# Both parts of each mixer weight kept in DRAM for the second token half, and W_down added up into four output blocks

## The chip, the cores and the metric

The kernel runs on one core of a Trainium2 chip. The metric is device time in microseconds (us); lower is better. PE is TensorE (matmuls), DVE is VectorE, ACT is ScalarE, POOL is GpSimd, and SP is SyncE, which here only issues DMA transfers, one after the other, in a fixed order.

## The reference

One decoder layer on x of 1024 tokens by 1024 columns, in float32:

```python
h    = rms_norm(x, norm_mix_pre)
proj = h @ w_in                      # 1024 x 2568: u, v (gMLP), z, xBC (Mamba-2), dt
y_a  = u * (W_s @ layer_norm(v) + b) # per chunk of 128 tokens, after gelu
y_b  = ssd(conv(xBC), dt) * silu(z)  # chunked scan over 128-token chunks, then normed
x    = x + rms_norm(concat[y_a, y_b] @ w_out, norm_mix_post)
f    = relu(rms_norm(x, norm_ffn_pre) @ w_up) ** 2     # 1024 x 4096
x    = x + rms_norm(f @ w_down, norm_ffn_post)
```

## The kernel before

Every float32 product is made of three matmuls in the faster type float32r (`mm3`): an operand is cut into a high part (an ACT cast) and a low part (a subtraction, on POOL or DVE; `split`), and high x high, high x low and low x high are added up in PSUM.

**Mixer (0 to about 440 us).** Tokens go in two halves of 512, H0 and H1. Weights come in units of 512 KB. The list `units` has 28 mixer units (8 for xBC, 4 for z, 4 for v, 4 for u, 8 for `w_out`) and names each of them twice, once for each half; then 16 units of `w_up`. `load_unit` (line 216) loads a unit into one of two staging tiles `ws`, ACT casts it to `wh`, POOL subtracts to `wl`, and both stand in a ring of five (`N_SPLIT`) until PE has used them. The second use of a unit repeats all of this. The scan part works chunk by chunk: `ssd_a` loads a tile `gg` of decay sums by SP (`gg<-acd`, line 582), DVE, ACT and DVE turn it into a mask, and PE uses it in `ssd_c`. PE fills the time between chunks with the z, v and u products.

**W_up (440 to 750 us)** and **W_down (750 to 1018 us)** use Strassen's scheme with seven products instead of eight for blocks of 2 x 2. W_down works on 7 groups of `f` rows in stages `SG` of one, two, two and two groups. In a stage the seven products come in the order `ORD`; each is added up in one of two sets of four PSUM banks (`pd`), and product 2 goes on top of product 1, product 3 on top of product 5 (`MORE`). After each product `flush` (line 1184) adds the bank set to one of seven SBUF blocks `acc` of 128 x 2048. Behind the last stage, further adds between these blocks make four output blocks out of seven.

**Tail (1018 us to the end).** The eighth group is multiplied plainly, for 8 token tiles (t) in two column halves each, 12 matmuls into a bank `pl`: DVE adds `pl` to `acc`, ACT squares and sums, POOL multiplies by the norm weight, DVE runs a chain of small operations for 1/rms (`chain`), and `finish` scales, adds x and writes out. `TAIL` sets which tiles share a chain: three pairs, then two single tiles. `some(k)` sets how many steps of the chain and finish of an earlier tile are issued after each `pl` add.

All engines run their instructions in order. In the mixer the order on each engine is set by a scheduler at build time; the tail is in written order.

Of the kernel before, what the change touches and what calls it, by code (L numbers as in the profile page):

```python
# [8 lines left out]
F32 = mybir.dt.float32  # L9
# [6 lines left out]
P = 128  # L16
# [40 lines left out]
def hymba_kernel(ctx, tc, x, norm_mix_pre, w_in, gm_ln_w, gm_ln_b, gm_w_s, gm_b_s,  # L57
# [151 lines left out]
    def stage_unit(i):  # L209
# [3 lines left out]
        loads.append(nc.sync.dma_start(st, src).ins.name)  # L213
        staged[i] = st, shape

    def load_unit(eng=None):
        i = state["load"]
        if i >= len(units):
            return
        state["load"] += 1  # L220
        if i not in staged:
            stage_unit(i)
        st, shape = staged.pop(i)
        wh = wpool.tile(shape, F32R, tag="wh", bufs=N_SPLIT, name=f"wh{i}")
        wl = wpool.tile(shape, F32R, tag="wl", bufs=N_SPLIT, name=f"wl{i}")
        split(wh, wl, st, eng)
        ready.append((wh, wl))

    def next_unit(ahead=2, eng=None):
        i = state["use"]  # L230
# [114 lines left out]
    def step(op):  # L345
        kind, arg = op[0], op[1:]
        t = int(arg[0]) if arg else 0
        if kind == "S":
            ssx[t] = sumsq(x0[t], f"ssx0{t}")
        elif kind == "R":  # L350
            chains = [rstd_steps(ssx[int(c)], D) for c in arg]
            for c, steps in zip(arg, chains):
                rx[int(c)] = next(steps)
            while chains:
                chains = [c for c in chains if next(c, 0) is None]
        elif kind == "N":
            dve.scalar_tensor_tensor(x0[t], x0[t], rx[t], wpre, op0=ALU.mult, op1=ALU.mult)
        elif kind == "M":
            for q in range(2):
                qs = slice(q * 512, (q + 1) * 512)  # L360
                pool.tensor_tensor(x0[t][:, qs], x0[t][:, qs], wpre[:, qs], op=ALU.mult)
        elif kind == "C":
            act.activation(x0[t], x0[t], AF.Copy, scale=rx[t])
        elif kind == "T":
            for q in range(2):
                ps = (mm_bank, ss_bank, mi_bank)[PRO_BANK[t]](f"tx0{t}_{q}")
                psx[t, q] = ps.rearrange("p (k c) -> p k c", c=P)
                for k in range(4):
                    c0 = (4 * q + k) * P
                    pe.transpose(psx[t, q][:, k, :], x0[t][:, c0:c0 + P], ident)  # L370
        elif kind in "HL":
            q = int(arg[1])
            h, l = [y[:, 4 * q:4 * q + 4, t * P:(t + 1) * P] for y in hT]
            if kind == "H":
                act.copy(h, psx[t, q])
            else:
                dve.tensor_tensor(l, psx[t, q], f(h), op=ALU.subtract)
        elif kind == "W":
            st, shape = staged.pop(t)
            wh = wpool.tile(shape, F32R, tag="wh", bufs=N_SPLIT, name=f"wh{t}")  # L380
            wl = wpool.tile(shape, F32R, tag="wl", bufs=N_SPLIT, name=f"wl{t}")
            act.copy(wh, st)
            units01[t] = wh, wl, st
        elif kind == "V":
            wh, wl, st = units01[t]
            pool.tensor_tensor(wl, st, f(wh), op=ALU.subtract)
            ready.append((wh, wl))
            state["load"] += 1
        else:
            small_setup()  # L390
# [482 lines left out]
    def sub(eng, out_, a, b):  # L873
        tt(eng, out_, a, b, ALU.subtract)
# [219 lines left out]
    now["nwp"] = pool_of(ctx, "nw2")  # L1094
    pctx2 = stack()
    psum2 = pool_of(pctx2, "psum2", space=bass.MemoryType.PSUM)
    accs = {i: apool.tile([P, 4, 512], F32, name=f"acc{i}") for i in range(1, 8)}
    last = N_GROUP - 1


    SG = [(0,), (1, 2), (3, 4), (5, 6), (last,)]
    sg_of = {g: (n, gs.index(g)) for n, gs in enumerate(SG) for g in gs}
    ORD = (1, 5, 2, 3, 6, 7, 4)
    MORE = {2: 1, 3: 5}
    raws, wts, pcs = {}, {}, {}
    wr_loads = []

# [20 lines left out]
    def w_block(g, key):  # L1128
        if key[0] == "b":
            return rows(g, int(key[1]) - 1)[:, :, int(key[2]) - 1, :]  # L1130
        if (g, key) not in wts:
            one, two = {"t1": ("b12", "b11"), "t2": ("b22", "t1"), "t3": ("b22", "b12"),
                        "t4": ("t2", "b21")}[key]
            a_, b_ = w_block(g, one), w_block(g, two)
            t_ = a_ if key == "t4" else dpool.tile([P, 2, 512], F32, tag="wt", bufs=4, name=f"w{key}_{g}")
            sub(dve, t_, a_, b_)
            wts[g, key] = t_
        return wts[g, key]
# [3 lines left out]
    frs = {}  # L1142

    def f_load(name, src):
        frs[name] = stage.tile([P, 2, 512], F32, tag="ws", bufs=N_STAGE, name="fr" + name)
        nc.sync.dma_start(frs[name], src)

    def f_piece(name, tags=("fh", "fl"), bufs=3):
        fr = frs[name]
        hl = piece([P, 2, 512], "f" + name) if tags is None else \  # L1150
            tuple(dpool.tile([P, 2, 512], F32R, tag=t_, bufs=bufs, name=f"f{i}" + name)
                  for i, t_ in enumerate(tags))
        split(*hl, fr)
        return hl
# [26 lines left out]
    floads = [lambda g=g, i=i: d_load(g, i) for n, g, i in seq]  # L1181
    floads += [lambda i=i: last_load(i) for i in range(4)]

    def flush(n, i, ps):
        a_ = accs
        if n == 0:
            act.copy(a_[i], ps)
            return
        if n == len(SG) - 2 and i == 4:
            sub(dve, a_[4], a_[4], ps)  # L1190
            return
        add(dve, a_[i], ps, a_[i])
        if n < len(SG) - 2:
            return
        if i == 6:
            add(dve, a_[6], a_[6], a_[1])
            add(dve, a_[3], a_[3], a_[6])
        elif i == 7:
            add(dve, a_[7], a_[7], a_[6])
            sub(dve, a_[4], a_[7], a_[4])  # L1200
            add(dve, a_[5], a_[5], a_[7])

    w_load(0, 0)
    floads[0]()
# [5 lines left out]
    for m, (n, g, i) in enumerate(seq):  # L1210
        gs = SG[n]
        k = m - seq.index((n, gs[0], ORD[0]))
        if k == len(gs):
            w_load(n + 1, 0)
        elif k == 5 * len(gs) + 1:
            w_load(n + 1, 1)
        floads[m + 3]()
        preps[m + 2]()
        (fh, fl), (h, l) = pcs[g, i]
        if g == gs[0]:  # L1220
            banks[i] = banks[MORE[i]] if i in MORE else \
                psum2.tile([P, 4, 512], F32, tag="pd", bufs=2, name=f"pd{n}_{i}")
        ps = banks[i]
        for t in range(4):
            tsl = slice(t * P, (t + 1) * P)
            for q in range(2):
                mm3(ps[:, t, :], fh[:, q, tsl], fl[:, q, tsl], h[:, q, :], l[:, q, :],
                    g == gs[0] and q == 0 and i not in MORE, g == gs[-1] and q == 1,
                    skip_group_check=i in MORE)
        if g == gs[-1]:  # L1230
            flush(n, i, ps)
    for m in range(len(seq) + 2, len(preps)):
        if m + 1 < len(preps):
            floads[m + 1]()
# [4 lines left out]
    psum3 = pool_of(ctx, "psum3", space=bass.MemoryType.PSUM)  # L1239

    def acc(t, dh):
        return accs[((2, 3), (4, 5))[t // 4][dh]][:, t % 4, :]

    xqs, sss, chains, rs = [], {}, {}, {}
    TAIL = ((0, 1), (2, 3), (4, 5), (6,), (7,))

    def chain(ts):

        nsmall[0] += 1
        w = len(ts)  # L1250
        v = const.tile([P, w], F32, tag=f"tv{w}", bufs=2, name=f"tv{nsmall[0]}")
        dve.tensor_tensor(v, sss[ts][:, :, 0], sss[ts][:, :, 1], op=ALU.add)
        yield
        steps = rstd_steps(v, D)
        r = next(steps)
        for j, t in enumerate(ts):
            rs[t] = r[:, j:j + 1]
        yield from steps
# [38 lines left out]
    for ts in TAIL:  # L1297
        ss = sss[ts] = const.tile([P, len(ts), 2], F32, tag=f"st{len(ts)}", bufs=4, name=f"ssy{ts[0]}")
        for j, t in enumerate(ts):
            tsl = slice(t * P, (t + 1) * P)  # L1300
            for dh in range(2):
                ds_ = slice(dh * 512, (dh + 1) * 512)
                a_ = acc(t, dh)
                ps = psum3.tile([P, 512], F32, tag="pl", bufs=8, name=f"pl{t}{dh}")
                for i in range(4):
                    mm3(ps, ffs[i][0][:, tsl], ffs[i][1][:, tsl], us[i][0][:, dh, :],
                        us[i][1][:, dh, :], i == 0, i == 3)
                add(dve, a_, ps, a_)
                junk = now["tok"].tile([P, 512], BF16, tag="junk", bufs=1, name=f"yj{t}{dh}")
                act.activation(junk, a_, AF.Square, accum_out=ss[:, j, dh:dh + 1])  # L1310
                pool.tensor_tensor(a_, a_, wfpost[:, ds_], op=ALU.mult)
                some(6 if len(ts) > 1 else 12)
        todo.append(chain_op(ts))
        for t in ts:
            todo += [finish_op(t, 0), finish_op(t, 1)]
# [29 lines left out]
```

## Time and profile before

| | |
|---|---|
| Three timed runs | 1083.33, 1087.95, 1088.11 us; median 1087.95 |
| Profiled execution, own time | 1084.19 us |
| Its span, first to last instruction | 1082.5 us (so 1.7 us lie around it) |
| Busy share of PE, DVE, ACT, POOL | 95%, 70%, 46%, 36% |
| Mean granted TensorE clock | 0.983 |
| DMA moved | 172.40 MB, mean 159 GB/s |

Busy time is what an engine spent in instructions. PE is busy nearly all the time, so what counts is where PE stands still, what it waits for there, and what happens behind its last matmul. The granted clock is a share of TensorE's full 2.4 GHz: 0.50 in a stretch is the level of 1.2 GHz.

### The profile page before, as it was taken

What the parts mean: (1) busy time and instruction counts of PE and PEld (TensorE: products, weight loads), DVE (VectorE), ACT (ScalarE), POOL (GpSimd) and SP (SyncE); (2) the same over time, 40 slices, a digit from 0 to 9 for tenths busy, and PEclk for the clock granted to TensorE, in tenths of its full rate; (3) what the DMA queues carried; (4) which work ended last, traced back from release to release, by engine and by line L of the source; (5) the groups of instructions that cost most, each with busy time, mean ns of one, the idle gap of its engine ahead of it and who ended that gap; (6) DMA issues with size and microseconds to landing.
All of it is one profiled execution on the core that took longest, in us unless ns stands there. A gap on an engine that the chain in (4) does not pass through costs nothing.

```text
span 1082.5 us, 13146 instructions
## 1 busy us (share of the span) xinstructions
PE 1026.2 (95%) x4735; PEld 835.8 (77%) x4735; DVE 761.1 (70%) x1246; ACT 500.1 (46%) x673; POOL 389.0 (36%) x197
## 2 busy tenths in 40 slices
PE   5999997999899989999999999999999999999795
PEld 4877676777678878888788888887888888888684
DVE  5746887267986745668477777776758778767957
ACT  5546453353463533676444444445753333333221
POOL 5543525233545151500011111113444444444543
PEclk9999998999999999999999999999999999999898
DMA  6443412324852133766767777767654354434413
GB/s 199 135 120 134 153 43 78 107 68 139 260 169 76 40 117 98 227 220 193 244 195 230 226 225 229 227 220 254 249 191 172 96 173 134 143 108 172 152 39 116
DMA packets 139560, 172.40 MB, mean 159 GB/s; under 512 B 8308, under 2 KB 83176, under 8 KB 139496
## 3 DMA queue, kind: packets, MB, share of 16 engines
q1 hardware_dynamic: 105064, 152.70, 42.7%
q10 hardware_dynamic: 34432, 18.88, 6.0%
q8 instruction: 37, 0.61, 0.2%
q14 instruction: 27, 0.22, 0.1%
HBM read 129.05 MB, written 42.50 MB: 158 GB/s over the span
## 4 chain that ended last, share of the span: by engine, by line
PE 71%; DVE 16%; DMA 4%; ACT 4%; issue 3%; SPq 1%; POOL 1%; DVEq 0%; ACTq 0%
PE pd L73 22%; PE pe L73 8%; PE puC L73 8%; PE puB L73 8%; PE pso L73 8%; PE puD L73 4%; PE pl L73 3%; DVE v L73 3%; PE psv L73 2%; PE psz L73 2%; DMA gg<-acd 2%; DVE acc L73 2%; DVE gg L73 1%; PE psB L73 1%; DVE rt L73 1%
## 5 line engine op out<-in xcount | busy, mean ns | idle before, releaser
L73 POOL TENSOR_TENSOR wl<-ws,wh 128x1024 fp32r<-128x1024 f32 x64 | 160.6, 2516 | 209.3 <-ACT wh L73 198.1
L73 PE MATMUL pd<-whd,f 128*128 128x512 f32 x752 | 231.5, 389 | 0.0
L73 POOL TENSOR_TENSOR f<-fr,f 128x1024 fp32r<-128x1024 f32 x47 | 117.7, 2507 | 143.2 <-ACT f L73 134.9
L73 PEld LDWEIGHTS pd<-whd,f 128*128 128x128 f32 x752 | 141.2, 188 | 29.1
L73 PE MATMUL pd<-wld,f 128*128 128x512 f32 x376 | 146.3, 389 | 0.0
L73 POOL TENSOR_TENSOR wlb<-sa,whb 128x1024 fp32r<-128x1024 f32 x16 | 38.5, 2406 | 223.7 <-ACT whb L73 189.1
L73 ACT CAST f<-fr 128x1024 fp32r<-128x1024 f32 x47 | 49.4, 1054 | 137.8 <-PE pd L73 134.0
L73 ACT CAST wh<-ws 128x1024 fp32r<-128x1024 f32 x72 | 75.2, 1046 | 73.2 <-PE pso L73 14.4
L73 PEld LDWEIGHTS pd<-wld,f 128*128 128x128 f32 x376 | 70.6, 188 | 14.8
L73 DVE TENSOR_TENSOR wld<-wt,whd 128x1024 fp32r<-128x1024 f32 x28 | 60.8, 2173 | 27.0 <-ACT whd L73 22.9
L73 ACT ACTIVATE u<-u 128x512 f32<-128x512 f32 (+1 forms) x66 | 44.3, 672 | 54.1 <-DVE u L73 48.5
L73 DVE TENSOR_TENSOR wld<-wr,whd 128x1024 fp32r<-128x1024 f32 x21 | 46.3, 2205 | 28.4 <-ACT whd L73 28.4
L73 DVE TENSOR_TENSOR acc<-pd,acc 128x2048 f32<-128x2048 f32 x20 | 45.7, 2287 | 10.1 <-PE pd L73 10.1
L73 ACT ACT_TABLE_LOAD x30 | 38.5, 1283 | 30.8 <-DVE carry L73 8.1
L73 PE MATMUL pe<-hTh,wh 128*128 128x512 f32 x128 | 50.3, 393 | 0.0
L73 PE MATMUL pe<-hTh,wl 128*128 128x512 f32 x128 | 49.9, 390 | 0.0
L73 PE MATMUL pe<-hTl,wh 128*128 128x512 f32 x128 | 49.9, 389 | 0.0
L73 DVE TENSOR_TENSOR u<-puB,s 128x512 f32<-128x512 f32 x32 | 22.1, 691 | 31.9 <-PE puB L73 16.7
L73 DVE TENSOR_SCALAR gg<-gg,acs 128x128 f32<-128x128 f32 x64 | 21.2, 389 | 22.3 <-DMA gg<-acd 22.3
L73 DVE TENSOR_TENSOR wlc<-sa,whc 128x1024 fp32r<-128x1024 f32 x16 | 29.4, 1835 | 6.1 <-ACT whc L73 6.1
L73 PE MATMUL pso<-wh,mixbh 128*128 128x512 f32 x64 | 28.0, 438 | 4.2 <-DVE hTl L73 2.9
L73 ACT ACTIVATE f<-f 128x512 f32<-128x512 f32 x32 | 20.2, 633 | 25.0 <-DVE f L73 24.5
(345 smaller groups left out, 2706.5 us busy)
## 6 DMA issues: line engine op xcount, KB each, us to landing
fr<-fsp SPq DMA_DIRECT2D x49, 512.0 KB, 3.8
ws<-in_w_in_dram SPq DMA_DIRECT2D x40, 512.0 KB, 4.1
wu<-in_w_up_dram ACTq DMA_DIRECT2D x32, 512.0 KB, 4.2
wr<-in_w_down_dram SPq DMA_DIRECT2D x32, 512.0 KB, 5.9
fsp<-c SPq DMA_DIRECT2D x42, 256.0 KB, 2.0
ws<-in_w_out_dram SPq DMA_DIRECT2D x16, 512.0 KB, 3.3
ws<-in_w_up_dram SPq DMA_DIRECT2D x16, 512.0 KB, 4.2
fsp<-u SPq DMA_DIRECT2D x28, 256.0 KB, 3.3
```

Source lines behind the costliest of these rows:

```text
L73: ins = fn(*a, **k)
```

## The change

**Mixer.** At the first use of a unit, both parts are written to DRAM tiles `wd` right behind the split (`keep`, two writes of 512 KB). At the second use (`again`) the two parts are loaded from there straight into the ring: no staging tile, no cast, no subtraction.

**W_down.** There are four blocks `acc` (11, 12, 21, 22) from the start. Products 6, 7 and 4 are added on top of product 1 in the banks, product 3 on top of 5, and the blocks `INTO` take what stands in the banks after each product. The order of products is new, and the adds between blocks behind the last stage are gone. In the first stage the first flush into each block is an ACT copy (four), the others are DVE adds (three); before, all seven were ACT copies. The freed SBUF holds four more tiles for loads of `f` (tag `fr`) and a fourth pair of `f` parts.

**Tail.** Every token tile has its own chain, and the first column half's share of the mean is made ahead (`tbase`).

```diff
@@ load_unit, keep, again
+        if id(units[i]) in first:
+            again(i)
+            return
+        first[id(units[i])] = i
...
+        keep(i)
+
+    def keep(i):
+
+        if any(u is units[i] for u in units[i + 1:]):
+            parts[i] = [dram.tile([P, 1024], F32, name=f"wd{i}{j}") for j in range(2)]
+            for d, t_ in zip(parts[i], ready[i]):
+                nc.sync.dma_start(d, f(t_.rearrange("p a b -> p (a b)")))
+
+    def again(i):
+        shape = [P, 8, P] if units[i][0] == "m" else [P, 2, 512]
+        hl = [wpool.tile(shape, F32R, tag=t_, bufs=N_SPLIT, name=f"{t_}{i}") for t_ in ("wh", "wl")]
+        for d, t_ in zip(parts[first[id(units[i])]], hl):
+            ins = nc.sync.dma_start(f(t_.rearrange("p a b -> p (a b)")), d)
...
@@ W_down
-    ORD = (1, 5, 2, 3, 6, 7, 4)
-    MORE = {2: 1, 3: 5}
+    ORD = (1, 5, 6, 3, 7, 2, 4)
+    MORE = {6: 1, 3: 5, 7: 1, 4: 1}
+    INTO = {1: 11, 5: 22, 6: 12, 3: 12, 7: 22, 2: 11, 4: 21}
...
-        add(dve, a_[i], ps, a_[i])
-        if n < len(SG) - 2:
-            return
-        if i == 6:
-            add(dve, a_[6], a_[6], a_[1])
-            add(dve, a_[3], a_[3], a_[6])
-        elif i == 7:
-            add(dve, a_[7], a_[7], a_[6])
-            sub(dve, a_[4], a_[7], a_[4])
-            add(dve, a_[5], a_[5], a_[7])
+        a_ = accs[INTO[i]]
+        if INTO[i] in done:
+            add(dve, a_, ps, a_)
+        else:
+            act.copy(a_, ps)
+            done.add(INTO[i])
...
@@ tail
-    TAIL = ((0, 1), (2, 3), (4, 5), (6,), (7,))
+    TAIL = tuple((t,) for t in range(8))
...
+        if w == 1:
+            steps = rstd_steps(sss[ts][:, 0, 1:2], D, tbase[ts])
...
-                some(6 if len(ts) > 1 else 12)
+                some(7 if len(ts) > 1 else 10 if t == 7 and dh == 0 else 15)
+                if len(ts) == 1 and dh == 0:
+                    tbase[ts] = rstd_base(ss[:, 0, 0:1], D)
```

On SP, in the first token half around the first loads of `gg` (about 53 to 65 us; `ws` are loads of weight units, `acd` the decay sums that `gg` is loaded from), these transfers stood in a row before:

```order
L213 DMA ws_1037<-in_w_in_dram 128x8x128
L213 DMA ws_1070<-in_w_in_dram 128x8x128
L526 DMA acd_277<-acsT_405 32x128
L582 DMA gg_0_586<-acd_277 128x512
L582 DMA gg_0_608<-acd_277 128x512
L213 DMA ws_1103<-in_w_in_dram 128x2x512
```

At the same place of the change (the `wd` rows are the new writes of a high or low part):

```order
L213 DMA ws_1077<-in_w_in_dram 128x8x128
L241 DMA wd_872<-wh_868 128x1024
L550 DMA acd_285<-acsT_417 32x128
L241 DMA wd_873<-wl_869 128x1024
L213 DMA ws_1114<-in_w_in_dram 128x8x128
L241 DMA wd_1083<-wh_1079 128x1024
L606 DMA gg_0_610<-acd_285 128x512
L606 DMA gg_0_632<-acd_285 128x512
L241 DMA wd_1084<-wl_1080 128x1024
L213 DMA ws_1151<-in_w_in_dram 128x2x512
```

Two writes and one load now stand between the decay sums and the first `gg`, and each write waits for a cast or a subtraction.

On DVE, at the end of W_down (`acc` are the blocks, `pd` the banks, `wldl` the low parts of the eighth group's weights), before:

```order
L73 TENSOR_TENSOR acc_6473<-pd_6_8095,acc_6473 128x2048
L73 TENSOR_TENSOR wldl_8240<-wr_7868,whdl_8239 128x1024
L73 TENSOR_TENSOR acc_6473<-acc_6473,acc_6468 128x2048
L73 TENSOR_TENSOR acc_6470<-acc_6470,acc_6473 128x2048
L73 TENSOR_TENSOR wldl_8275<-wr_8195,whdl_8274 128x1024
L73 TENSOR_TENSOR acc_6474<-pd_7_8170,acc_6474 128x2048
L73 TENSOR_TENSOR wldl_8310<-wr_7868,whdl_8309 128x1024
L73 TENSOR_TENSOR acc_6474<-acc_6474,acc_6473 128x2048
L73 TENSOR_TENSOR acc_6471<-acc_6474,acc_6471 128x2048
L73 TENSOR_TENSOR acc_6472<-acc_6472,acc_6474 128x2048
L73 TENSOR_TENSOR wldl_8318<-wr_8195,whdl_8317 128x1024
L73 TENSOR_TENSOR acc_6471<-acc_6471,pd_4_8247 128x2048
```

And in the change:

```order
L73 TENSOR_TENSOR wldl_8281<-wr_7915,whdl_8280 128x1024
L73 TENSOR_TENSOR wldl_8315<-wr_8239,whdl_8314 128x1024
L73 TENSOR_TENSOR acc_6524<-pd_2_8214,acc_6524 128x2048
L73 TENSOR_TENSOR wldl_8350<-wr_7915,whdl_8349 128x1024
L73 TENSOR_TENSOR wldl_8358<-wr_8239,whdl_8357 128x1024
L73 TENSOR_TENSOR acc_6526<-pd_1_7853,acc_6526 128x2048
```

The five adds between blocks are gone, and all four low parts stand ahead of the last flush.

In the tail, DVE now has, between the adds of the last tile's two halves (`pl_8737`, `pl_8771`), the chain of tile 6 (9 rows), one finish and the base of tile 7. Behind the second add:

```order
L73 TENSOR_TENSOR acc_6527<-pl_8771,acc_6527 128x512
L73 SCALAR_TENSOR_TENSOR acc_6527<-acc_6527,rr_8755,wr_8373 128x512
L73 TENSOR_SCALAR rv_8790<-ssy_8736,rb_8769 128x1
L73 TENSOR_SCALAR rti_8793<-rv_8790 128x1
L73 TENSOR_SCALAR rr_8791<-rti_8793 128x1
```

Before, an addition (`tv`) stood ahead of `rv` there, and no finish.

## Rows read from the trace of the kernel before

**Rows 1.** Busy time by stretch: us, PE, PEld, DVE, ACT, POOL, PEclk, DMA, GB/s.

```profile
27.00:135.00 108.00, 102.54 (x550) 81.39 (x549) 73.75 (x197) 59.57 (x78) 49.48 (x33) 1.00 0.44 135
135.00:205.00 70.00, 62.88 (x303) 50.87 (x302) 46.74 (x93) 29.66 (x41) 25.08 (x14) 0.93 0.21 64
205.00:264.00 59.00, 56.64 (x255) 43.98 (x255) 33.56 (x103) 28.95 (x44) 18.16 (x11) 0.97 0.32 102
264.00:297.00 33.00, 29.38 (x137) 22.93 (x136) 32.90 (x81) 12.04 (x18) 18.55 (x10) 0.95 0.80 256
297.00:440.00 143.00, 139.27 (x685) 113.57 (x684) 92.90 (x235) 66.16 (x97) 56.05 (x28) 0.99 0.34 107
1018.00:1082.50 64.50, 45.14 (x191) 36.56 (x189) 44.67 (x95) 13.29 (x34) 27.56 (x18) 0.88 0.23 85
```

**Rows 2.** What PE waited for, whole run: us in total, times, longest.

```profile
PE pl L73 <- DVE acc L73: 6.3, 1, 6.3
...
PE pssp L73 <- DVE v L73: 2.8, 1, 2.8
...
PE psx L73 <- ACT wh L73: 0.2, 1, 0.2
```

**Rows 3.** Timeline of PE, tail: start, length, instruction, [idle before <- who ended it].

```profile
1017.58 0.39 PE L73 MATMUL pl<-whdl,f0l 128*128 128x512 f32 x1
...
1025.89 0.80 PE L73 MATMUL pl<-whdl,f0l 128*128 128x512 f32 x1 [6.34 <-DVE acc L73]
...
1066.60 0.39 PE L73 MATMUL pl<-whdl,f0l 128*128 128x512 f32 x1
...
1069.09 0.39 PE L73 MATMUL pl<-whdl,f1l 128*128 128x512 f32 x1
```

**Rows 4.** Timeline of DVE at the end of W_down.

```profile
1000.38 6.69 DVE L73 TENSOR_TENSOR acc<-acc,acc 128x2048 f32<-128x2048 f32 x2
...
1011.48 8.88 DVE L73 TENSOR_TENSOR acc<-acc,acc 128x2048 f32<-128x2048 f32 x3
...
1023.57 2.27 DVE L73 TENSOR_TENSOR acc<-acc,pd 128x2048 f32<-128x2048 f32 x1
```

**Rows 5.** Two stretches at the lower TensorE clock, columns as in rows 1.

```profile
384.10:387.50 3.40, 3.08 (x7) 2.52 (x8) 1.77 (x5) 2.11 (x3) 3.40 (x2) 0.51 0.73 258
1022.40:1029.20 6.80, 3.31 (x8) 2.63 (x9) 3.44 (x2) 1.04 (x1) 2.51 (x2) 0.50 0.01 2
```

**Rows 6.** Timeline of DVE, from the last add to the last finish.

```profile
1074.07 0.68 DVE L73 TENSOR_TENSOR acc<-pl,acc 128x512 f32<-128x512 f32 x1
1075.60 0.16 DVE L73 TENSOR_TENSOR tv<-ssy 128x1 f32<-128x1 f32 x1 [0.85 <-ACT yj L73]
1075.80 0.15 DVE L73 TENSOR_SCALAR rv<-tv 128x1 f32<-128x1 f32 x1
...
1078.11 1.41 DVE L73 SCALAR_TENSOR_TENSOR acc<-acc,rr,wr 128x512 f32<-128x512 f32 x2
```

**Rows 7.** Costliest groups of the page: busy us, mean ns | idle before, releaser.

```profile
L73 POOL TENSOR_TENSOR wl<-ws,wh 128x1024 fp32r<-128x1024 f32 x64 | 160.6, 2516 | 209.3 <-ACT wh L73 198.1
...
L73 ACT CAST wh<-ws 128x1024 fp32r<-128x1024 f32 x72 | 75.2, 1046 | 73.2 <-PE pso L73 14.4
...
L73 DVE TENSOR_TENSOR acc<-pd,acc 128x2048 f32<-128x2048 f32 x20 | 45.7, 2287 | 10.1 <-PE pd L73 10.1
```

**Rows 8.** Two DVE groups of one shape, 205 to 440 us, columns as in rows 7.

```profile
L73 DVE TENSOR_TENSOR v<-v,lnb 128x512 f32<-128x512 f32 x4 | 6.3, 1592 | 0.0
...
L73 DVE TENSOR_TENSOR v<-v,lnw 128x512 f32<-128x512 f32 x4 | 2.5, 681 | 0.0
```

**Rows 9.** DMA issues of the page: count, KB each, us from issue to landing.

```profile
gg<-acd SPq DMA_DIRECT2D x16, 256.0 KB, 4.3
...
x2d<-o SPq DMA_DIRECT2D x8, 512.0 KB, 4.3
```

**Rows 10.** Busy time in the first stage of W_down, columns as in rows 1.

```profile
752.00:790.00 38.00, 36.31 (x159) 29.55 (x158) 27.65 (x19) 27.69 (x24) 21.18 (x7) 1.00 0.63 231
```

More of the change, by code (lines that the diff above doesn't have):

```diff
@@ L214, in stage_unit @@
         staged[i] = st, shape
+    first, parts = {}, {}
     def load_unit(eng=None):
@@ L227, in load_unit @@
         ready.append((wh, wl))
+        keep(i)
[9 more added lines that the diff above has]
+            ins = nc.sync.dma_start(f(t_.rearrange("p a b -> p (a b)")), d)
+        loads.append(ins.ins.name)
+        ready.append(tuple(hl))
     def next_unit(ahead=2, eng=None):
@@ L387, in step @@
             ready.append((wh, wl))
+            first[id(units[t])] = t
+            keep(t)
             state["load"] += 1
@@ L1096, in hymba_kernel @@
     psum2 = pool_of(pctx2, "psum2", space=bass.MemoryType.PSUM)
-    accs = {i: apool.tile([P, 4, 512], F32, name=f"acc{i}") for i in range(1, 8)}
+    accs = {k: apool.tile([P, 4, 512], F32, name=f"acc{k}") for k in (11, 12, 21, 22)}
     last = N_GROUP - 1
@@ L1132, in w_block @@
             one, two = {"t1": ("b12", "b11"), "t2": ("b22", "t1"), "t3": ("b22", "b12"),
-                        "t4": ("t2", "b21")}[key]
+                        "t4": ("b21", "t2")}[key]
             a_, b_ = w_block(g, one), w_block(g, two)
-            t_ = a_ if key == "t4" else dpool.tile([P, 2, 512], F32, tag="wt", bufs=4, name=f"w{key}_{g}")
+            t_ = b_ if key == "t4" else dpool.tile([P, 2, 512], F32, tag="wt", bufs=4, name=f"w{key}_{g}")
             sub(dve, t_, a_, b_)
@@ L1144, in f_load, with f_piece @@
     def f_load(name, src):
-        frs[name] = stage.tile([P, 2, 512], F32, tag="ws", bufs=N_STAGE, name="fr" + name)
+        pool_, tag, bufs = (stage, "ws", N_STAGE) if len(frs) < N_CARRY else (dpool, "fr", 4)
+        frs[name] = pool_.tile([P, 2, 512], F32, tag=tag, bufs=bufs, name="fr" + name)
         nc.sync.dma_start(frs[name], src)
-    def f_piece(name, tags=("fh", "fl"), bufs=3):
+    def f_piece(name, tags=("fh", "fl"), bufs=4):
         fr = frs[name]
@@ L1182, in hymba_kernel, with flush @@
     floads += [lambda i=i: last_load(i) for i in range(4)]
[L1184 to L1187, printed above, removed]
-            return
-        if n == len(SG) - 2 and i == 4:
-            sub(dve, a_[4], a_[4], ps)
-            return
-        add(dve, a_[i], ps, a_[i])
-        if n < len(SG) - 2:
-            return
-        if i == 6:
-            add(dve, a_[6], a_[6], a_[1])
-            add(dve, a_[3], a_[3], a_[6])
-        elif i == 7:
-            add(dve, a_[7], a_[7], a_[6])
-            sub(dve, a_[4], a_[7], a_[4])
-            add(dve, a_[5], a_[5], a_[7])
+    done = set()
+    def flush(i, ps):
+        a_ = accs[INTO[i]]
[4 more added lines that the diff above has]
+            done.add(INTO[i])
     w_load(0, 0)
@@ L1221, in hymba_kernel @@
             banks[i] = banks[MORE[i]] if i in MORE else \
-                psum2.tile([P, 4, 512], F32, tag="pd", bufs=2, name=f"pd{n}_{i}")
+                psum2.tile([P, 4, 512], F32, tag=f"pd{(n + (i != 1)) % 2}", bufs=1, name=f"pd{n}_{i}")
         ps = banks[i]
@@ L1230, in hymba_kernel @@
         if g == gs[-1]:
-            flush(n, i, ps)
+            flush(i, ps)
     for m in range(len(seq) + 2, len(preps)):
@@ L1241, in acc @@
     def acc(t, dh):
-        return accs[((2, 3), (4, 5))[t // 4][dh]][:, t % 4, :]
+        return accs[((11, 12), (21, 22))[t // 4][dh]][:, t % 4, :]
     xqs, sss, chains, rs = [], {}, {}, {}
-    TAIL = ((0, 1), (2, 3), (4, 5), (6,), (7,))
+    TAIL = tuple((t,) for t in range(8))
+    tbase = {}
     def chain(ts):
@@ L1250, in chain @@
         w = len(ts)
+        if w == 1:
+            steps = rstd_steps(sss[ts][:, 0, 1:2], D, tbase[ts])
+            rs[ts[0]] = next(steps)
+            yield from steps
+            return
         v = const.tile([P, w], F32, tag=f"tv{w}", bufs=2, name=f"tv{nsmall[0]}")
```

## The prediction

> **What bounds the kernel now.** I read the busy times first, then what PE waited for, then the places themselves. PE is busy 95% of the span, so time can be won only where PE stands still, where its clock is low, or behind its last matmul. By stretch [rows 1], PE stands still in the first token half for 108 - 102.54 = 5.5 us (27 to 135 us) and 7.1 us (135 to 205), 12.6 together; in the second half for 2.4, 3.6 and 3.7 us, 9.7 together. The granted clock there is 0.97, 0.95 and 0.99, which costs 59 x 0.03 + 33 x 0.05 + 143 x 0.01 = 4.9 us more. From 1018 us to the end PE works 45.1 of 64.5 us at clock 0.88: the tail is the worst stretch.
>
> The waits of PE say why [rows 2]. The longest is 6.3 us, once, a `pl` matmul that DVE keeps waiting through `acc`. The mixer's named wait is 2.8 us, `pssp` for DVE's `v`. For a weight part PE waited 0.2 us in all, and no row names POOL's `wl`. So the splits that the change removes never hold PE up by themselves: what they give must come through another engine.
>
> In the tail [rows 3] PE starts at 1017.58, stops at once for 6.34 us, and ends its last matmul at about 1069.5. There are 192 matmuls (8 tiles, 2 halves, 12 each); the last bank's lie (1069.09 - 1066.60) / 11 = 0.226 us apart, so the tail needs 43.5 us of PE, and a tile 5.43. The stop is made on DVE [rows 4]: five adds between blocks, 6.69 us for two and 8.88 for three, push the flush of product 4 to 1023.57, and PE goes on when it ends. Behind the stop the clock is 0.50 for 6.8 us, the lower of the two levels [rows 5]; PE was busy 3.31 us there, half of which, 1.65, is lost. At the end [rows 6] DVE makes its last add at 1074.07, 4.6 us behind PE's last matmul; from there to the end of the span it is 8.4 us (ACT, `tv`, the chain, two finishes, the write).
>
> **The change, part by part.**
>
> *W_down's blocks and the tail.* The five adds are gone: 15.6 us of DVE. The bank set of product 2 is flushed while PE makes product 4, which needs more than the 2.27 us of a flush [rows 4], so the first `pl` bank is free when PE comes. Stop 6.3 and clock 1.65 go: -8.0. Late next would be product 4's own flush, but PE needs that bank set only after four half tiles of 2.7 us each, 10.9 us later.
> DVE's lag behind PE's last matmul comes from the 6.3 us and from pair chains. Per tile, from [rows 6], DVE has now two adds of 0.68, a chain of 78.11 - 75.80 = 2.31, two finishes of 1.41 together and a base of about 0.15 (a 128x1 step, as `rv`): 5.2 us, against PE's 5.43. DVE just keeps up. Between the last tile's adds stand tile 6's chain, one finish and the base, 2.31 + 0.70 + 0.15, and the add itself is 0.68: 3.8 us against the 2.7 us that PE needs for the half, so the last add ends 1.1 us late instead of 4.6: -3.5. `tv` without its rest, 0.2: -0.2. Sum -11.7. Bounds: if DVE lags by 0.5 us more in each tile, the 3.5 are lost and the sum is about -8; with ACT late as well, -7; with no lag at all, -13.
> Stage 0 of W_down now has three DVE adds of 2.29 us [rows 7]. DVE was busy 27.65 of 38 us there [rows 10], so 34.5 fits: 0, hidden by PE's 36.31 us. If the flush stands behind DVE work that itself waits for loads, PE waits for the bank set: up to +3.
>
> *Second half of the mixer.* 28 subtractions of 2.516 us on POOL and 28 casts of 1.046 on ACT [rows 7] go, 70 and 29 us of engines that PE does not wait for. What they do to others is seen on DVE [rows 8]: two groups of the same shape, adding `lnb` and multiplying by `lnw`, take 1592 and 681 ns. No operand explains it; the slow ones ran while POOL subtracted. Four times 0.91 is 3.6 us, just ahead of the 2.8 us that PE waited for `v`; behind that wait the clock was 0.51 for 3.4 us [rows 5], 1.5 us of PE work lost. I count the wait and the clock, 4.3, in full, and of the remaining 9.7 + 4.9 - 4.3 = 10.3 us of idle and clock a quarter, 2.6, since other DVE work is stretched too but PE's wait for it is not in sight: -7 (bounds 0, POOL was only a bystander, and -14.6, all of it).
> The Trainium skill (SBUF — State Buffer, "SBUF: two separate sides") says that a DVE operation with two SBUF inputs and a GpSimd operation take a shared port pair in turn, each for its whole length. The 1592 against 681 ns agree; by that rule alone the gain would lie toward -14.6.
> The second loads move 28 x 0.52 = 14.7 MB more in 235 us, 63 GB/s. From 135 to 256 GB/s the DMA share goes from 0.44 to 0.80 [rows 1], 0.003 per GB/s: +0.19, which makes 0.99 in the worst stretch (264 to 297) and about 0.5 elsewhere. A unit is wanted every 235 / 28 = 8.4 us and is two transfers of 4.3 [rows 9]; with five ring places the load can run some 30 us ahead. 0.
>
> *First half of the mixer.* 56 writes of 512 KB are added, 29.4 MB. Between 27 and 135 us POOL's 49.48 us hold at most 19 subtractions; I take 17 units, 17.8 MB in 108 us, +165 GB/s: the share rises from 0.44 to about 0.94. SP issues in order, and a write waits for its cast or subtraction; behind it wait weight loads and the eight loads of `gg` (half of the 16 in [rows 9]), which DVE's masks and then PE's `ssd_c` wait for. A `gg` took 4.3 us to land [rows 9]. Below: 0, if z, v and u products cover it, as they cover it now. Above: +12.6, the idle time doubled. I take +3, a quarter, nearer to zero because PE waited 0.2 us for weights [rows 2].
>
> Sum on the span: 1082.5 - 11.7 - 7 + 3 = 1066.8; with the 1.7 us around it 1068.5, against the profiled run's own 1084.19. The runs go from 1083.33 to 1088.11, median 1087.95, 3.8 above the profiled one. I go halfway, since the median rests on three: **1070.5 us**.
>
> **The rivals.** The measurement can tell about 0.5%, 5.4 us, from no change: 1082.5 to 1093.4 is "same".
> - *A, both parts pay*: the sum above, 1061 to 1075. Chance 0.60.
> - *B, only the tail pays*, the mixer nets nothing: for it speaks that PE never waited for `wl`. 1082.5 - 11.7 (or -8) + 1.7, and the halfway 1.9: 1074 to 1078, and to 1082 if the writes take 4. Chance 0.18.
> - *C, no change to be seen*: DVE becomes the bound of the tail, 5.2 against 5.43 us per tile being close, so that it gives 8, and the writes take 8 or more while the second half gives little: 1082.5 - 8 + 8 + 3.6 = 1086. Chance 0.11.
> - *D, slower*: the transfers stand in line, and each `gg` pays for what is now ahead of it. Two writes and a load of 4.3 us each stand between the decay sums and `gg`: 12.9 us; with half of it covered by other products, 6.5 x 8 = 52 us, and 1068.5 + 49 + 1.9, about 1119. It is slower than "same" from (18.7 + 5.4) / 8 = 3.0 us uncovered per `gg`. For it: the share of 0.94. Against it: PE has products of z, v and u to put between. [...] Chance 0.08.
> - *E, more than A*: DVE's freedom from POOL gives all 14.6 and the writes nothing: 1082.5 - 11.7 - 14.6 + 3.6 = 1060, or under. Chance 0.03.
>
> **How the numbers follow.** Faster by over 0.5% are A, most of B and E: 0.79. Same: 0.13 (C, the end of B and the mild end of D). Slower: 0.08. The forecast is A's. The range for 8 in 10 takes A and B, and reaches up to where C begins and down to E: 1059 to 1083.
>
> **What would show it.**
> - Tail: PE's wait for `acc` is at most 0.5 us and the clock is 1.00 behind W_down; the last add ends at most 1.5 us behind the last matmul. A wait of `pl` on DVE in every tile would show C.
> - Second half: POOL's busy time is 70 us less, ACT's 29 less, adding `lnb` takes about 0.7 us, the wait of `pssp` is under 0.5, and PE stands still 4 to 6 us from 205 to 440, not 9.7. If `lnb` falls to 0.7 and the idle time stays, B holds.
> - First half: the DMA share is near 0.9; PE's idle time is 16 us or less of the 12.6 before plus the 3; `gg` lands within 7 us. Landing times of 10 us or more with PE waiting on a mask show D.
> - Stage 0: PE's wait for banks is 3 us or less.
> The prediction fails most easily in the first half: its price is the one that no row of before holds.

## The result and the profile after

The change runs in 1072.49 us (median of 4, 1070.68 to 1074.90) against 1087.65 us of before (median of 4, 1083.33 to 1088.11): ratio 0.9869, 95% interval 0.9836 to 0.9902. The forecast was 1070.5 us, range 1059 to 1083.

The profiled run of the change has a span of 1073.1 us and an own time of 1074.9, the slowest of its four; that of before lies below its median. So the two traces differ by 9.4 us where the medians differ by 15.2. What follows divides the 9.4 and does not say where the rest lies. From the timelines of PE and DVE:

| us | before | after | difference |
|---|---|---|---|
| PE's first product of the second token half (`psB`) | 211.77 | 216.37 | +4.6 |
| PE's first W_up product | 435.89 | 427.40 | -8.5 |
| PE's first W_down product | 748.75 | 741.24 | -7.5 |
| PE's first tail product | 1017.58 | 1019.95 | +2.4 |
| PE's last matmul | 1069.09 | 1063.25 | -5.8 |
| DVE's last add | 1074.07 | 1064.65 | -9.4 |
| end of the span | 1082.5 | 1073.1 | -9.4 |

The place that parts the token halves, before and after:

```profile
211.77 0.39 PE L73 MATMUL psB<-hTh,wh 128*128 128x512 f32 x1
```

```profile
216.37 0.40 PE L73 MATMUL psB<-hTh,wh 128*128 128x512 f32 x1
```

The mixer gives 8.5 us (the first token half costs 4.6, the second gives 13.1) and the tail 11.8 (8.2 to PE's last matmul, 3.6 from there to DVE's last add), but W_down takes 9.9 back. Busy time by stretch of the change (us, PE, PEld, DVE, ACT, POOL, PEclk, DMA share, GB/s; cut at 205 us as in [rows 1], else at places of the table):

```profile
27.00:205.00 178.00, 164.04 (x838) 132.62 (x837) 122.52 (x288) 84.38 (x115) 67.14 (x42) 0.95 0.72 247
205.00:427.40 222.40, 220.08 (x1073) 178.00 (x1072) 137.06 (x402) 86.41 (x134) 27.20 (x23) 1.00 0.58 207
...
741.24:1019.95 278.71, 269.99 (x1177) 222.39 (x1176) 208.05 (x104) 111.14 (x109) 129.02 (x51) 0.98 0.47 163
1019.95:1063.60 43.65, 43.65 (x193) 35.84 (x191) 34.15 (x97) 10.87 (x30) 18.72 (x15) 1.00 0.21 83
...
773.20:783.40 10.20, 5.55 (x13) 4.39 (x14) 10.16 (x6) 0.00 (x0) 4.61 (x2) 0.50 0.42 137
```

In the second half PE stands still 222.40 - 220.08 = 2.3 us at clock 1.00, where [rows 1] had 9.7 us and clocks of 0.95 to 0.99. In the tail PE has no idle time and full clock. In the first half PE stands still 14.0 us against 12.6 in [rows 1], at clock 0.95. What PE waited for in the change, the longest waits of the run but for the start's two of `tx` (us in total, times, longest):

```profile
PE pd L73 <- DVE acc L73: 7.9, 1, 7.9
PE pso L73 <- DVE hTl L73: 5.3, 2, 4.0
PE psC L73 <- DVE gg L73: 3.3, 1, 3.3
```

The wait of `pl` for `acc` in [rows 2] is gone; a longer one, of `pd` for `acc`, has come. It is in the first stage of W_down. Timelines of DVE and POOL there (start, length, instruction):

```profile
761.10 1.21 DVE L73 TENSOR_TENSOR wld<-wr,whd 128x1024 fp32r<-128x1024 f32 x1
762.23 3.42 DVE L73 TENSOR_TENSOR wld<-wt,whd 128x1024 fp32r<-128x1024 f32 x1
765.58 3.43 DVE L73 TENSOR_TENSOR wt<-wr,wt 128x1024 f32<-128x1024 f32 x1
768.93 3.39 DVE L73 TENSOR_TENSOR wld<-wr,whd 128x1024 fp32r<-128x1024 f32 x1
772.24 3.36 DVE L73 TENSOR_TENSOR wt<-wr,wt 128x1024 f32<-128x1024 f32 x1
775.52 2.28 DVE L73 TENSOR_TENSOR acc<-pd,acc 128x2048 f32<-128x2048 f32 x1
```

```profile
761.07 16.74 POOL L73 TENSOR_TENSOR f<-fr,f 128x1024 fp32r<-128x1024 f32 x5 [4.39 <-ACT f L73]
```

DVE works without a gap, and the flush of product 3 (the row at 775.52) is last in line. The same kind of operation takes 1.21 us at 761.10, where it starts together with POOL's first subtraction, and about 3.4 us in the four rows after it, and these four lie inside the 16.74 us in which POOL subtracts five `f` parts back to back. PE has finished product 3 at about 764.6 us and product 7, in the other bank set, at about 769.9. It starts product 2 at 777.85, when the flush ends, 7.95 us late, and its clock is at the lower level from 773.2 to 783.4 us, in which it works 5.55 us, half of that lost: 7.9 + 2.8 = 10.7 us, less 0.9 us of a shorter wait for a low part at the stage's start. That is W_down's +9.9.

### The profile page after: what moved, and what is told of

It reads as the page before. It is cut to its first block, busy times and chain, and to the rows that moved or that the text cites. A ratio compares the mean times of both kernels' runs of the same rounds, so it can differ in the third digit from the quotient of the medians.

```text
span 1073.1 us, 13234 instructions
## 1 busy us (share of the span) xinstructions
PE 1023.7 (95%) x4735; PEld 836.4 (78%) x4735; DVE 743.8 (69%) x1265; ACT 468.6 (44%) x642; POOL 313.3 (29%) x169
## 5 line engine op out<-in xcount | busy, mean ns | idle before, releaser
L73 PE MATMUL pd<-whd,f 128*128 128x512 f32 x752 | 234.2, 392 | 7.9 <-DVE acc L73 7.9
L73 POOL TENSOR_TENSOR wl<-ws,wh 128x1024 fp32r<-128x1024 f32 x36 | 87.7, 2440 | 191.9 <-ACT wh L73 191.7
L73 DVE TENSOR_TENSOR wld<-wt,whd 128x1024 fp32r<-128x1024 f32 x28 | 63.5, 2267 | 26.9 <-ACT whd L73 26.9
L73 ACT CAST wh<-ws 128x1024 fp32r<-128x1024 f32 x44 | 46.1, 1049 | 53.1 <-DMA ws<-in_w_in_dram 17.5
L73 DVE TENSOR_TENSOR acc<-pd,acc 128x2048 f32<-128x2048 f32 x24 | 54.9, 2287 | 14.8 <-PE pd L73 14.8
L73 ACT CAST whd<-wt 128x1024 fp32r<-128x1024 f32 x28 | 29.3, 1046 | 5.7 <-DVE wt L73 2.8
```

Source lines behind the costliest of these rows:

```text
L73: ins = fn(*a, **k)
```

## The experiments

Ratios are to the kernel before on the same chip.

**Which part gives what.** The mixer part alone, then the W_down and tail part alone:

```diff
 (e1_mixer_only: everything behind the W_up part as before)
-    ORD = (1, 5, 6, 3, 7, 2, 4)
+    ORD = (1, 5, 2, 3, 6, 7, 4)
...
 (e2_down_only: no keep, no again)
-        keep(i)
...
```

> The mixer part of the change alone; W_down and the tail as before. Theory: the two parts add up. By the traces the change brings PE to the first W_up product 8.5 us earlier (435.9 to 427.4 us), so this kernel is 8 to 9 us faster than before, ratio about 0.992, and its tail shows the 6.3 us wait of pl again. Rival: the parts depend on each other (what is won in the mixer is lost in W_up or W_down, whose loads come at other moments): less than 3 us faster.

Measured: 1078.32 us, ratio 0.9915 (0.9888 to 0.9942); PE's first W_up product at 428.2 us.

> The W_down and tail part of the change alone; mixer as before. Theory: in the first stage of W_down PE waits 6 to 9 us for a bank set, because the flush of product 3 is now a DVE add that stands in DVE's queue behind weight sums and low parts; with the lower clock behind it this eats nearly all of what the tail gives, and the kernel is only 1 to 3 us faster than before. Rival: the wait came from the mixer part (W_down's row loads or weight parts late after the added transfers): no such wait here, and the kernel is about 11 us faster than before.

Measured: 1079.98 us, ratio 0.9941 (0.9919 to 0.9964). What PE waited for, of the first and of the second kernel:

```profile
PE pl L73 <- DVE acc L73: 6.3, 1, 6.3
```

```profile
PE pd L73 <- DVE acc L73: 8.0, 1, 8.0
```

The mixer's share came out as expected, and the new wait belongs to the W_down part: the mixer's writes and loads have no part in it. That part alone still gained 6.5 us of median where 1 to 3 were expected; its profiled run, the slowest of its seven, is 3.5 us below that of before, and where the rest lies is not seen. The two gains, 0.85% and 0.59%, add up to 1.44%, the change's 1.31% within the intervals.

**The wait for the bank set: three ways at it.** First another engine for the one flush:

```diff
...
-        if INTO[i] in done:
+        if n == 0 and i == 3:
+            act.copy(accs[21], ps)
+            add(dve, a_, a_, accs[21])
+        elif INTO[i] in done:
```

> The whole change, but product 3 of the first stage is copied by ACT into block 21, which is free until product 4, and DVE adds block 21 to block 12 later. Theory: PE waits only for the bank set, not for DVE's sum, so the 7.9 us wait and the lower clock behind it go: 8 to 11 us faster than the change, about 1062 to 1065 us. Rival: DVE as a whole is late in this stage, so PE waits for a low part of weights (pd for wld) in place of the bank set: under 3 us faster than the change.

Measured: 1072.79 us, ratio 0.9882 (0.9852 to 0.9912), as the change. Waits of PE, and DVE's timeline:

```profile
PE pd L73 <- DVE acc L73: 10.2, 1, 10.2
```

```profile
768.16 3.41 DVE L73 TENSOR_TENSOR wt<-wr,wt 128x1024 f32<-128x1024 f32 x1
771.50 4.43 DVE L73 TENSOR_TENSOR acc<-acc,acc 128x2048 f32<-128x2048 f32 x1
775.85 3.36 DVE L73 TENSOR_TENSOR wld<-wr,whd 128x1024 fp32r<-128x1024 f32 x1
779.13 2.28 DVE L73 TENSOR_TENSOR acc<-pd,acc 128x2048 f32<-128x2048 f32 x1
```

My theory fell. ACT's copy did free the bank set early, at about 763 us, but one product later PE needed the next flush, product 7's, and that one stood behind the same stretched rows and the extra add. The rival was nearer: DVE as a whole is late; but PE waited for a flush again, not for a low part. So why is DVE late: for what it was given, for the order it works in, or for POOL? The load tiles of `f` first:

```diff
-        pool_, tag, bufs = (stage, "ws", N_STAGE) if len(frs) < N_CARRY else (dpool, "fr", 4)
+        pool_, tag, bufs = (stage, "ws", N_STAGE) if len(frs) < N_CARRY else (stage, "ws", N_STAGE)
```

> The whole change, but loads of f go through the two staging tiles as before the change, in place of the four new tiles fr. Theory: with four more tiles POOL runs five f subtractions in a row from 761 to 778 us, and DVE's sums and low parts beside them take 3.4 us in place of 1.2; with two tiles POOL's subtractions come spaced, DVE's backlog shrinks by some 6 us or more, PE's wait for the bank set falls from 7.9 to under 3 us, and the kernel is 5 to 10 us faster than the change. Rival: the three adds of 2.3 us that ACT's copies gave up to DVE make the backlog; then the wait stays at 6 to 8 us and the time at that of the change.

Measured: 1061.49 us, ratio 0.9773 (0.9750 to 0.9796); PE waits for `acc` nowhere. The order on PE and POOL is that of the change; DVE's and ACT's differ in a few rows, but 15 DVE rows of the stage stand ahead of the flush in both. DVE and POOL at the same place:

```profile
760.12 1.22 DVE L73 TENSOR_TENSOR wt<-wr,wt 128x1024 f32<-128x1024 f32 x1
761.26 3.43 DVE L73 TENSOR_TENSOR wld<-wr,whd 128x1024 fp32r<-128x1024 f32 x1
764.61 2.28 DVE L73 TENSOR_TENSOR acc<-pd,acc 128x2048 f32<-128x2048 f32 x1
766.82 1.23 DVE L73 TENSOR_TENSOR wld<-wr,whd 128x1024 fp32r<-128x1024 f32 x1
```

```profile
760.32 6.65 POOL L73 TENSOR_TENSOR f<-fr,f 128x1024 fp32r<-128x1024 f32 x2 [4.73 <-ACT f L73]
768.49 2.41 POOL L73 TENSOR_TENSOR f<-fr,f 128x1024 fp32r<-128x1024 f32 x1 [1.52 <-ACT f L73]
```

POOL now has two subtractions in a row, not five, one DVE row ahead of the flush is stretched here in place of four, and the flush starts at 764.61, some 11 us earlier, though the stage begins only 3.6 us earlier. All three DVE adds are still there, so they are not the cause by themselves. Then the order alone, with the four tiles kept:

```diff
+    dve.held = True
     w_load(0, 0)
...
             flush(i, ps)
+            if m == 6:
+                dve.held = False
```

> The whole change, but DVE keeps the written order in the first stage of W_down, so that the flush of product 3 stands four rows earlier, ahead of sums and low parts for the next stage. Theory: these rows are needed only by later products, so the wait of 7.9 us falls by their 13 us to near nothing, and the kernel is 6 to 10 us faster than the change. Rival: DVE is late as a whole and some of these rows are needed at once: PE waits as long at the next product, for a low part or the next flush, as it did where the flush of product 3 was taken over by ACT; under 3 us faster.

Measured: 1064.77 us, ratio 0.9792 (0.9765 to 0.9818). PE's wait:

```profile
PE pd L73 <- DVE acc L73: 3.2, 3, 1.8
```

With the flush ahead of sums that later stages need, the 7.9 us fall to 3.2 in three pieces, and the lower clock goes. W_down, from its first product to the tail's first, takes 278.7 us in the change, 271.7 here, and 268.8 with two tiles, as before the change. The loss thus needs both: POOL's subtractions in a row, and the flush placed behind the stretched rows. Two load tiles take it all away, the earlier flush most of it. The fourth pair of `f` parts was there in both, so it is not the cause by itself.

**Why the second half gains.** Subtractions put back on POOL that nobody waits for:

```diff
         ready.append(tuple(hl))
+        st = stage.tile(shape, F32, tag="ws", bufs=N_STAGE, name=f"no{i}")
+        pool.tensor_tensor(st, f(hl[0]), f(hl[1]), op=ALU.subtract)
```

> The whole change, with 28 subtractions put back on POOL in the second token half: each reads the two loaded parts of a unit and writes a free staging tile that nobody reads. Theory: POOL's subtractions cost by stretching DVE's operations; adding lnb goes from 0.68 back to 1.2 to 1.6 us, PE stands still 5 us or more longer between 205 and 427 us, and the kernel is 5 to 10 us slower than the change. Rival: the second half gains because weight parts no longer pass ACT and POOL; then these subtractions, which nothing waits for, cost under 2 us.

Measured: 1081.16 us, ratio 0.9947 (0.9928 to 0.9965), 8.7 us above the change. Busy time of its second half, and two DVE groups there, then the mask group in the second half of the change:

```profile
205.00:431.00 226.00, 219.51 (x1051) 176.07 (x1050) 153.09 (x401) 85.58 (x133) 90.17 (x48) 0.98 0.58 206
```

```profile
L73 DVE TENSOR_SCALAR gg<-gg,acs 128x128 f32<-128x128 f32 x32 | 14.3, 507 | 6.2 <-DMA gg<-acd 6.2
...
L73 DVE TENSOR_TENSOR v<-v,lnb 128x512 f32<-128x512 f32 x4 | 2.6, 680 | 0.0
```

```profile
L73 DVE TENSOR_SCALAR gg<-gg,acs 128x128 f32<-128x128 f32 x32 | 7.0, 280 | 6.8 <-DMA gg<-acd 6.8
```

DVE has the same work as in the change (401 and 402 instructions) and needs 153.1 us for it in place of 137.1; the mask group takes 507 ns, in the change 280 and before it 458. PE stands still 6.5 us in place of 2.3. That supports the theory over the rival. One detail was wrong: adding `lnb` stayed at 680 ns, since POOL's work now lay beside other operations, and PE waited in the scan (`psC` and `psB` for DVE's `xg`, 2.0 and 1.2 us) in place of `pssp`. The profiled run, 1076.15 us, is the fastest of its ten, and reaches the first W_up product only 3.6 us behind the change. But its first half was 4.8 us shorter (`psB` at 211.61 us), without the lower clock at 128 us. From `psB` to the first W_up product it takes 219.4 us, the change 211.0 (five other kernels with the same mixer 211.0 to 212.6) and the kernel before 224.1. So in the second half the subtractions cost 8.4 us against the change, the size of the 8.7, and are 8.4 of the 13.1 us gained there.

**What the writes cost.** Almost no writes, then half of them with the casts back on ACT:

```diff
 (e7_no_writes)
-        if any(u is units[i] for u in units[i + 1:]):
+        if not parts:
...
-        for d, t_ in zip(parts[first[id(units[i])]], hl):
+        for d, t_ in zip(parts[0], hl):
 (e8_low_only, in keep and in again)
-            for d, t_ in zip(parts[i], ready[i]):
-                nc.sync.dma_start(d, f(t_.rearrange("p a b -> p (a b)")))
+            nc.sync.dma_start(parts[i], f(ready[i][1].rearrange("p a b -> p (a b)")))
...
+        if i not in staged:
+            stage_unit(i)
+        st, _ = staged.pop(i)
+        act.copy(hl[0], st)
+        nc.sync.dma_start(f(hl[1].rearrange("p a b -> p (a b)")), parts[first[id(units[i])]])
```

> The whole change without 54 of the 56 writes: only the first unit's two parts are written, and every second use loads these two (so the second token half is multiplied by wrong weights). Theory: the writes cost the first half what the traces differ by there, 1.4 us of idle time and 4.0 us of lower clock, so this kernel is 4 to 6 us faster than the change, and PE stands still about 12.5 us from 27 to 205 us. Rival: the first half differs for another reason (the order that the schedule gives it): within 2 us of the change.

Measured: 1066.52 us, ratio 0.9816 (0.9789 to 0.9842), 6.0 us below the change.

> The whole change, but only the low parts go to DRAM: the second use loads the unit as before, ACT casts the high part, and the low part is loaded; 28 writes in place of 56, no subtractions on POOL in the second half, the 28 casts on ACT stay. Theory: what the second half gains comes from POOL's absence, and what the first half loses from the writes: second half as fast as in the change (PE stands still 2 to 4 us from 205 us to W_up), first half 2 to 3 us better, so 0 to 4 us faster than the change. Rival: the casts on ACT matter too: second half loses half of its 12 us, and the kernel is 3 us or more slower than the change.

Measured: 1068.11 us, ratio 0.9830 (0.9808 to 0.9852), 4.4 us below the change. Busy time of the first half, e7 and then e8, and e8's second half:

```profile
27.00:205.00 178.00, 166.65 (x861) 132.95 (x861) 118.30 (x289) 85.08 (x117) 66.58 (x42) 0.98 0.40 125
```

```profile
27.00:205.00 178.00, 165.38 (x870) 132.18 (x869) 121.40 (x288) 89.41 (x121) 66.72 (x42) 1.00 0.57 186
205.00:422.27 217.27, 214.60 (x1041) 173.62 (x1040) 135.24 (x401) 106.11 (x155) 28.30 (x23) 0.99 0.59 197
```

The theories held as far as the intervals let one tell (both reach into the change's by a little): by the medians the writes cost 4 to 6 us, and 20 us more of casts on ACT leave PE's second half nearly as it is (2.7 us idle; 213.0 us from `psB` to W_up, against 211.0 in the change).

How far single traces carry here is seen at `psB`. It comes at 211.6 to 216.8 us in the seven kernels that write both parts, at 208.6 to 212.8 in the three that write low parts alone (e8 and two below), at 210.0 with almost no writes, and at 211.2 and 211.8 in the two with the mixer of before. A difference of 4 us between two traces is thus within the spread of the same first half. What parts the groups is PE's wait for a mask (`psC` for `gg`): 2.5 to 4.3 us in the seven, 0.8 to 1.2 in the six others. In the change the first `gg` was issued 5.3 us behind the decay sums (64.1 and 69.4 us), before it 3.6 us behind them (60.2 and 63.8). And the first mask's first rows on DVE, of the change and then of before:

```profile
73.84 2.33 DVE L73 TENSOR_SCALAR gg<-gg,acs 128x128 f32<-128x128 f32 x4 [7.30 <-DMA gg<-acd]
```

```profile
67.18 0.87 DVE L73 TENSOR_SCALAR gg<-gg,acs 128x128 f32<-128x128 f32 x4 [8.36 <-DMA gg<-acd]
```

In the change they ran beside a subtraction on POOL (73.12 to 75.50 us). So part of the wait is POOL's stretching again, not the late transfer. The order on all engines also differs between these kernels, since the scheduler sets it anew; the runs don't part that from the traffic.

**The tail's chains as before:**

```diff
-    TAIL = tuple((t,) for t in range(8))
+    TAIL = ((0, 1), (2, 3), (4, 5), (6,), (7,))
...
```

> The whole change, but the tail's chains as before (three pairs, then two single tiles, with the addition tv and without the bases made ahead). Theory, the prediction's term for DVE's lag: single chains with a base keep the last add within 1.5 us of PE's last matmul; with pairs it is 2 to 4 us later, and the kernel 2 to 4 us slower than the change. Rival: the lag of before came from the 6.3 us stop, and with it gone pairs do as well: the last add ends within 2 us of PE, and the time is within 1 us of the change.

Measured: 1077.43 us, ratio 0.9915 (0.9895 to 0.9935), by the medians 4.9 us above the change, a little more than expected, with intervals that just touch; the traces are clear. PE's last matmul and DVE's last add:

```profile
1061.64 0.39 PE L73 MATMUL pl<-whdl,f1l 128*128 128x512 f32 x1
```

```profile
1065.33 1.42 DVE L73 SCALAR_TENSOR_TENSOR acc<-acc,rr,wr 128x512 f32<-128x512 f32 x2
1066.66 0.69 DVE L73 TENSOR_TENSOR acc<-pl,acc 128x512 f32<-128x512 f32 x1
```

The add stands 5.0 us behind the start of the last matmul, as before the change, where it was 1.4 with single chains: the lag came from the pairs, not from the stop. From the tail's first product to the end this trace takes 57.0 us, the change 53.2.

**The cures together:**

```diff
 (e10_low_fr: the edits of e8 and of e5; e11_low_fr_first: that of e6 too)
```

> Low parts alone in DRAM and f loaded through the staging tiles: the two cures together, the first for the first token half, the second for the first stage of W_down. Theory: they lie in different places and add up, 4 and 11 us, so about 1057 us, and neither the 7.9 us wait for a bank set nor the lower clock before 205 us is there. Rival: with other orders and phases the lock of POOL and DVE comes back in the first stage (a wait of 3 us or more for acc), and the time stays at 1060 to 1066 us.

Measured: 1060.46 us, ratio 0.9771 (0.9746 to 0.9797).

> The same with DVE in written order in the first stage of W_down. Theory: the flush's place in DVE's queue no longer matters once DVE is not behind, so this is within 2 us of the kernel with the two cures. Rival: an early flush still gains a wait of 1 us or more there, or costs one by making a low part late; then the two differ by 3 us or more.

Measured: 1059.17 us, ratio 0.9753 (0.9727 to 0.9780). Neither kernel waits for `acc`, and the first shows no lower clock before 205 us, but its 1057 were not reached: it is as fast as e5 (0.9771 and 0.9773), so the edit of e8, which gave 4.4 us beside the four tiles, shows no gain beside two. In the profiles the first gains 3.9 us on e5 by the first W_up product, within the spread given above; a wait of 1.7 us for a low part in W_down's first stage (at 742 us, e5's at 745) is followed by the lower clock only in the first, where W_down takes 1.6 us longer, and W_up 0.6. Beyond that the missing gain stays open. The last is the fastest kernel of the study, below the change clear of both intervals; from e5 and e10 it can't be told.

## Why the prediction was right, and where it was wrong

The time was inside the range and 2 us from the forecast, and that closeness is in part luck: terms were wrong in opposite directions, and on the spans, from which the sum was made, it gave -15.7 us where the traces show -9.4. The medians differ by 15.2. By the terms of the sum, in the profiled spans:

- **Tail, -11.7: right in size and mechanism.** The stop and its clock gave 8.2 (8.0 predicted), the lag 3.6 (3.5). `tv` gave nothing: from the last add to the end it is 8.4 us as in [rows 6].
- **Second half, -7: right in mechanism, too small.** From `psB` to the first W_up product idle time fell from 9.7 to 2.3 us, and PE's busy time by 5.7, since the lower clock went: 13.1 us, near the bound of -14.6. The step that failed is the quarter I took for waits without a name. One of them had a name, in a line of the waits of before that [rows 2] leaves out:

```profile
PE psC L73 <- DVE rr L73: 3.0, 2, 2.8
```

The longer of the two waits, 2.8 us, ends at 287.8 us, in the second half. It is as long as the `pssp` wait, has 3.4 us of lower clock behind it, and is gone in the change. (Nor was the wait of 6.3 us the longest: at the start two waits of `tx` made 12.1.) By e4, POOL's work stretched other work of DVE too, the mask group among it, not only what stood ahead of `v`. The Trainium skill (SBUF — State Buffer, "SBUF: two separate sides") says that a DVE operation with two SBUF inputs and a GpSimd operation take the shared ports in turn. The 1.21 against 3.42 us agree with it; by it alone this term would have been nearer, the time would not.

- **First half, +3: too small in this pair of traces, within its bounds.** From 27 us to `psB`, 4.6 us: 1.4 of idle time, and 3.2 by which PE's busy time grew, with the lower clock. I had priced idle time alone. The clock fell behind three waits (80, 128 and 179 us) where it fell once before. Over the seven traces with these writes `psB` lies 0 to 5 us behind that of before, so how much too small stays open.
- **Stage 0 of W_down, 0 with a bound of +3: wrong, +9.9 with its clock.** 27.65 + 6.9 us of DVE fitted in 38 us on average [rows 10], but the flush stood behind work that POOL stretched: PE wanted the bank set again at 769.9 us and the flush began at 775.5. I had named a flush behind DVE work that waits for loads; here DVE waited for nothing and was itself slow. I had used the stretching of [rows 8] as a gain in the mixer and not asked where the change brings POOL and DVE together anew: the four `fr` tiles were in the diff.
- W_up took 1.0 us more, which I did not trace.

Of the rivals, D did not come: one `gg` kept PE waiting 3.3 us (1.1 before), not each of eight, and the landings took 3.7 us in the middle and 5.0 at most. No run shows a `gg` held up behind a write once it was issued; what moved was when SP issued it. C's mechanism, a DVE bound in the tail, is not there either.

## What to carry to other kernels

When a change gives an engine more buffers, ask beside which other engine's work its instructions will now run in a row; here DVE's sums took three times as long beside POOL's, and a flush that frees a bank belongs ahead of work for later products. An average that fits a stage says nothing of the moment at which a bank set is wanted. Storing only what is expensive to make again (here the low part) kept the second half's gain; it was 4.4 us faster in one pair of kernels and no faster in another, so what it takes back of the writes' cost stays open.

## What the runs showed of the hardware

- DVE's 128x1024 sums took 1.21 us alone and 3.36 to 3.43 us beside POOL's subtractions, and POOL's took 3.35 us each (16.74 for five) where one alone took 2.41: both ran at one rate, as if each waited for nearly the whole of the other's operation (1.21 + 2.41 = 3.62).
- A 128x2048 add of two SBUF blocks took 4.43 us beside POOL (e3), against 2.96 to 3.35 in [rows 4], where POOL worked beside them part of the time; a flush with one operand in PSUM took 2.28 beside POOL in the change (775.52, inside POOL's 16.74 us).
- In the change, PE's waits of 3.3, 2.7, 4.0 and 7.9 us (ending at 79, 129, 179 and 778 us) each came with 3.4 to 10.2 us at the lower clock (0.50). A wait of 1.7 us in W_down's first stage was followed by it in e10 and not in e5.
